# A gated DeltaNet kernel on one core: an urgency for each stage of a unit, norm weights spread by TensorE, and the first and last state products left out

## The chip, the cores and the metric

The kernel runs on one core of a Trainium2 chip. The metric is the device time of one execution in microseconds (us), as the median of three runs. The kernel before takes 1268.69 us (1267.94 to 1268.84).

## The reference, cut to what matters

A model dimension of 1024, 2048 tokens, one layer of a gated DeltaNet with 8 heads of 128, and a final RMSNorm. Everything is float32. The parts that the change touches are the first norm and the chunked recurrence:

```python
h = x + gated_deltanet_mixer(rms_norm(x, a_norm_w), ...)   # then rms_norm(h, final_norm_w)

proj = h @ w_in                                   # q, k, v, z, and two gates per head
qkv  = silu(causal_depthwise_conv(qkv, conv_w))   # 4 taps
...
def step(state, xs):                              # one chunk of one head
    u_c, w_c, qd_c, kend_c, attn_c, gend_c = xs
    v_new = u_c - w_c @ state
    o_c = qd_c @ state + attn_c @ v_new
    state = state * gend_c[..., None, None] + jnp.swapaxes(kend_c, -1, -2) @ v_new
    return state, o_c

s0 = jnp.zeros((b_, h_, dk, dv), jnp.float32)
_, o = lax.scan(step, s0, (u, w, q_decayed, k_to_end, attn_intra, g_end))
y = rms_norm(o, o_norm_w) * silu(z)               # then y @ w_out
```

The state starts at zero, and the state after the last chunk is not an output. (The kernel uses chunks of 128 tokens.)

## The kernel before, in words

The work is cut into 16 units: 2 halves of the sequence (1024 tokens each) times 8 heads. A unit has these stages, each a function of its own. `project` (line 649) multiplies the normalised tokens by the head's slice of the weights, for k, q, v and z (KI, QI, VI, ZI), in two blocks of 512 tokens each. Tokens and weights are each split into a rounded part and its remainder (xh and xl, hi and lo), so a block of one kind is 24 matmuls of 512 columns. `conv_block` (622) does the convolution and SiLU. `decay` (664) makes the decay matrices, `k_side` (678) what depends on k and q alone, `invert` (723) the triangular inverse V, mostly as a long chain of small VectorE steps followed by four rounds of small matmuls, `v_side` (778) turns v, and `recur` (789) runs the 8 chunks of the recurrence one after the other, each reading the state S that the chunk before it left.

Ahead of unit 0 and again ahead of unit 8, `phase0` (512) loads and normalises the half's eight tiles of 128 tokens (`norm_tile`, 481), transposes them on TensorE and splits them; `gates` (543) follows. In `norm_tile` an even tile is scaled by one VectorE instruction (scale and norm weight at once), an odd one by ScalarE (scale) and then GpSimd (norm weight). After unit 15, `out_tile` (863) multiplies by the output weights; its first tiles are woven into the last units.

None of this is issued as it is written. Every call goes into a `Plan` (line 20), which records the operation with its dependencies and with `nc.prio`, the number set last before the call. `Plan.schedule` (193) then runs a list scheduler over the recorded operations with a cost table of its own: whenever an engine is free by its reckoning, it takes the ready operation with the lowest number (ties go to the one recorded first), unless a buffer is missing or the operation is more than `AHEAD` = 2.0 behind the most urgent one that is left. What comes out is one fixed order for each engine, and the engines keep to it. So `nc.prio` does not say when something runs. It only sets the order in each engine's queue, and a wrong reckoning shows as a wait of an engine for the head of its queue.

Before, the numbers are the unit's own number u for nearly everything of unit u, and u - 0.5 for `invert` and for the second half's norm and gates (lines 915 to 937):

```python
nc.prio = float(u)
...
nc.prio = u - 0.5
invert(un)
nc.prio = float(u)
project(un, ((VI, 0), ...))
v_side(un)
```

`recur(prev)` of unit u - 1 is recorded in round u with number u. Every instruction is emitted by line 354, so the profile's rows are told apart by their tiles: `xh,rnd` and `xl,rnd` are projections (rnd holds weights), `ident,big` transposes of the normalised tokens, `S`, `rho` and `n` belong to the recurrence (S is the state, `n` and `rho` are a chunk's intermediate results), `T` and `V` to the inverse, `half` is any tile of 512 columns, `bank` any PSUM bank. A float32 matmul stands in the trace as two instructions, one for each pass; a projection (float32r) as one.

## Time and profile before

| what | before |
|---|---|
| median of three runs | 1268.69 us |
| the profiled execution, its own time | 1271.77 us |
| its span, first to last instruction | 1270.0 us |
| TensorE (PE) busy | 1242.9 us |
| VectorE (DVE) busy | 954.2 us |
| ScalarE (ACT) busy | 615.5 us |
| GpSimd (POOL) busy | 173.0 us |
| mean granted TensorE clock | 0.988 |

The profiled execution's span is 1.3 us above the median of the runs. Busy time of PE includes the time in which one matmul drains while the next one already runs, so a stretch with 100% may still hold short waits. The granted clock has two levels, 1.00 (2.4 GHz) and 0.50 (1.2 GHz); a value in between is a mean over a stretch.

### The profile page before, as it was taken

The numbers are of one execution on the slowest core, as the hardware profiler recorded it, in microseconds if no ns is written. First come the engines' busy times: TensorE is split into PE (matmuls) and PEld (weight loads), VectorE is DVE, ScalarE is ACT, GpSimd is POOL, SyncE is SP. The second block draws the span as 40 slices with busy tenths as digits, with TensorE's granted clock in tenths as the row PEclk, the third lists the DMA queues.
The fourth block names the chain that finished last, engine by engine and source line by source line (L and its number), as shares of the span: only waits on it lengthen the run. The fifth ranks groups of instructions, "written<-read, shape, count | busy, mean of one in ns | idle before, by whom it ended". The sixth has DMA issues, their size and how long they took to land.

```text
span 1270.0 us, 21157 instructions
## 1 busy us (share of the span) xinstructions
PE 1242.9 (98%) x8093; PEld 1039.9 (82%) x8093; DVE 954.2 (75%) x2229; ACT 615.5 (48%) x1301; POOL 173.0 (14%) x277
## 2 busy tenths in 40 slices
PE   6999999999999999989999999999999999999997
PEld 5788788888888888878888888888888888888886
DVE  5678867887877869776787878787878698965653
ACT  6664364545455445556554545454545455232221
POOL 5211011101112102130110202020202010100000
PEclk9999899999999999989999999999999999999999
DMA  7130313122242131313302222222223316255721
GB/s 223 34 114 24 107 43 104 51 80 83 63 112 77 49 93 48 121 42 102 113 3 77 61 78 61 78 62 78 61 77 111 110 60 211 96 201 190 277 100 67
DMA packets 127623, 118.80 MB, mean 94 GB/s; under 512 B 24001, under 2 KB 106530, under 8 KB 127522
## 3 DMA queue, kind: packets, MB, share of 16 engines
q1 hardware_dynamic: 127522, 117.45, 30.3%
q8 instruction: 63, 1.03, 0.3%
q14 instruction: 38, 0.31, 0.1%
HBM read 98.36 MB, written 19.07 MB: 92 GB/s over the span
## 4 chain that ended last, share of the span: by engine, by line
PE 96%; DVE 2%; ACT 1%; DMA 0%; issue 0%; POOL 0%; SPq 0%; POOLq 0%; DVEq 0%; ACTq 0%
PE bank L354 96%; DVE half L354 1%; DMA big<-in_a_norm_w_dram 0%; DVE big L354 0%; ACT xh L354 0%; DVE xl L354 0%; ACT half L354 0%; POOL big L354 0%; DVE X L354 0%; ACT rnd L354 0%; DVE rnd L354 0%; ACT big L354 0%; SPq L354 0%; ACT n L354 0%; DVE sumo L354 0%
## 5 line engine op out<-in xcount | busy, mean ns | idle before, releaser
L354 PE MATMUL bank<-xh,rnd 128*128 128x512 f32 (+1 forms) x2624 | 884.1, 405 | 2.8 <-ACT rnd L354 1.7
L354 PEld LDWEIGHTS bank<-xh,rnd 128*128 128x128 f32 x2624 | 485.0, 190 | 91.5 <-ACT rnd L354 1.9
L354 PE MATMUL bank<-xl,rnd 128*128 128x512 f32 (+1 forms) x1328 | 535.0, 403 | 0.8 <-DVE xl L354 0.8
L354 PEld LDWEIGHTS bank<-xl,rnd 128*128 128x128 f32 x1328 | 253.4, 191 | 44.9 <-DVE xl L354 1.5
L354 DVE SCALAR_TENSOR_TENSOR half<-raw,vcol,half 128x512 f32<-128x512 f32 x288 | 211.8, 746 | 39.2 <-ACT half L354 37.0
L354 ACT ACTIVATE half<-half 128x512 f32<-128x512 f32 x128 | 81.6, 638 | 99.8 <-DVE half L354 98.2
L354 ACT CAST rnd<-big 128x1024 fp32r<-128x1024 f32 x80 | 83.8, 1050 | 76.3 <-PE bank L354 64.2
L354 ACT COPY raw<-bank 128x512 f32<-128x512 f32 x96 | 56.5, 588 | 118.9 <-PE bank L354 118.2
L354 ACT ACTIVATE n<-bank,nb 128x128 f32<-128x128 f32 x128 | 46.9, 366 | 131.2 <-PE bank L354 131.0
L354 DVE TENSOR_TENSOR rnd<-big,rnd 128x1024 fp32r<-128x1024 f32 x80 | 97.7, 1221 | 17.0 <-ACT rnd L354 14.2
L354 DVE TENSOR_TENSOR half<-X,big 128x6 f32<-128x6 f32 (+15 forms) x256 | 94.2, 368 | 4.4
L354 DVE TENSOR_REDUCE X<-half 128x2 f32<-128x6 f32 (+15 forms) x256 | 91.9, 359 | 3.7
L354 DVE SCALAR_TENSOR_TENSOR S<-S,dend,bank 128x128 f32<-128x128 f32 x128 | 44.1, 344 | 61.1 <-PE bank L354 60.2
L354 POOL COPY halo<-raw 128x3 f32<-128x3 f32 x72 | 21.5, 299 | 478.8 <-ACT raw L354 478.8
L354 ACT ACTIVATE half<-big 128x512 bf16<-128x512 f32 (+1 forms) x48 | 37.0, 772 | 81.5 <-issue 38.5
L354 ACT ACTIVATE half<-raw,vcol 128x512 f32<-128x512 f32 x96 | 69.6, 725 | 6.2 <-DVE vcol L354 1.5
L354 DVE SCALAR_TENSOR_TENSOR rho<-bank,eg,half 128x128 f32<-128x128 f32 x128 | 44.2, 345 | 25.6 <-PE bank L354 25.0
L354 PEld LDWEIGHTS bank<-rho,V 128*128 128x128 f32 x256 | 47.8, 191 | 11.9 <-ACT V L354 0.8
L354 PEld LDWEIGHTS bank<-n,half 128*128 128x128 f32 x256 | 47.5, 190 | 11.4 <-ACT n L354 1.4
L354 PEld LDWEIGHTS bank<-S,half 128*128 128x128 f32 x256 | 47.2, 191 | 11.2 <-DVE S L354 1.7
L354 POOL TENSOR_TENSOR sk<-ssk,phalf 128x4 f32<-128x4 f32 x32 | 39.5, 1233 | 123.2 <-DVE ssk L354 123.2
L354 ACT ACT_TABLE_LOAD x42 | 53.9, 1283 | 1.5 <-PEq L968 0.7
(114 smaller groups left out, 1583.2 us busy)
## 6 DMA issues: line engine op xcount, KB each, us to landing
big<-in_a_w_in_dram SPq DMA_DIRECT2D x64, 512.0 KB, 4.5
big<-in_x_dram SPq DMA_DIRECT2D x32, 512.0 KB, 4.1
big<-gd SPq DMA_DIRECT2D x16, 512.0 KB, 6.3
half<-gd SPq DMA_DIRECT2D x32, 256.0 KB, 4.3
big<-d SPq DMA_DIRECT2D x16, 512.0 KB, 5.4
yd<-half SPq DMA_DIRECT2D x32, 256.0 KB, 2.3
big<-yd SPq DMA_DIRECT2D x16, 512.0 KB
big<-rd SPq DMA_DIRECT2D x16, 512.0 KB, 4.5
```

The lines of the kernel that those rows point to most:

```text
L354: ins = getattr(getattr(self.tc.nc, op[6]), op[7])(*args, **kwargs)
```

## The change

There are three edits. First, each stage gets a number of its own relative to u, from a table `AT`; the projections of z are recorded separately from those of v, with u - 0.58, and weight loads get another -0.14. In the last unit of a half the gates get u - 0.31 in place of u - 0.5. Second, `a_norm_w` is no longer loaded into all 128 partitions by a DMA that reads the row 128 times. One row is loaded into partition 0, two matmuls with a row of ones spread it over the partitions, and two VectorE copies bring it back from PSUM. This holds for the first half; the second half's norm loads the weights as before. With it go smaller edits to the start: the first eight tiles are all scaled by VectorE, the very first in two halves. Third, the chunk that starts from the zero state (chunk 0 of units 0 to 7) issues no k S, no S qe, and copies instead of updating S, and the states are no longer cleared; the last chunk of units 8 to 15 doesn't update S at all.

```diff
+AT = dict(kq0=-0.25, kq1=-0.09, decay=0.0, k0=0.0, k1=-0.07, inv=-0.36, v=0.0, z=-0.58, vside=-0.67, phase=-0.5,
+          gates=-0.31, w=-0.14)
...
-    nws = [weights_row(a_norm_w)]
+    nc.prio = -1.1
+    ones = cp.tile([P, P], F32, name="ones")
+    nc.vector.memset(ones, 1.0)
+    nws = [st([P, D], F32, "nw")]
+    nc.sync.dma_start(nws[0][0:1], a_norm_w)
+    for c0 in range(0, D, TB):
+        pw = ps("nt")
+        nc.tensor.matmul(pw, lhsT=ones[0:1], rhs=nws[0][0:1, c0:c0 + TB], start=True, stop=True)
+        nc.vector.tensor_copy(nws[0][:, c0:c0 + TB], pw)
...
-    for h in range(H):
-        nc.gpsimd.memset(state[h], 0.0)
...
-        if t % 2:
+        if t % 2 and i >= len(x_first):
             nc.scalar.mul(xt, xt, rs)
             nc.gpsimd.tensor_tensor(out=xt, in0=xt, in1=nw, op=ALU.mult)
         else:
-            nc.vector.scalar_tensor_tensor(out=xt, in0=xt, scalar=rs, in1=nw, op0=ALU.mult, op1=ALU.mult)
+            for c0 in range(0, D, TB if i == 0 else D):
+                cols = slice(c0, c0 + (TB if i == 0 else D))
+                nc.vector.scalar_tensor_tensor(out=xt[:, cols], in0=xt[:, cols], scalar=rs, in1=nw[:, cols],
+                                               op0=ALU.mult, op1=ALU.mult)
...
+        at = nc.prio
+        if at >= 1:
+            nc.prio = at + AT["w"]
         nc.sync.dma_start(raw, w_in[:, c0:c0 + P].rearrange("(k p) c -> p k c", p=P))
         split_w(raw, hi, lo)
+        nc.prio = at
...
+            begin, end = un["sb"] == 0 and cc == 0, un["sb"] == NSB - 1 and cc == C - 1
             pch = ps("ch", (P, 3, P))
-            nc.tensor.matmul(pch[:, 0, :], lhsT=k[:, cs], rhs=S, start=True, stop=True)
             rho = st([P, P], F32, "rho")
-            nc.vector.scalar_tensor_tensor(out=rho, in0=pch[:, 0, :], scalar=gt["eg"][:, h, cc:cc + 1], in1=vp[:, cs],
-                                           op0=ALU.mult, op1=ALU.subtract)
+            if begin:
+                nc.vector.tensor_scalar_mul(rho, vp[:, cs], -1.0)
+            else:
+                nc.tensor.matmul(pch[:, 0, :], lhsT=k[:, cs], rhs=S, start=True, stop=True)
+                nc.vector.scalar_tensor_tensor(out=rho, in0=pch[:, 0, :], scalar=gt["eg"][:, h, cc:cc + 1],
+                                               in1=vp[:, cs], op0=ALU.mult, op1=ALU.subtract)
             nc.tensor.matmul(pch[:, 1, :], lhsT=V[:, cc, :], rhs=rho, start=True, stop=True)
             n = st([P, P], F32, "n")
             nc.scalar.mul(n, pch[:, 1, :], un["nb"][:, cc:cc + 1])
-            nc.tensor.matmul(po[:, c * P:(c + 1) * P], lhsT=S, rhs=qe[:, cs], start=True, stop=False)
-            nc.tensor.matmul(pch[:, 2, :], lhsT=kend[:, cs], rhs=n, start=True, stop=True)
-            nc.vector.scalar_tensor_tensor(out=S, in0=S, scalar=gt["dend"][:, h, cc:cc + 1], in1=pch[:, 2, :],
-                                           op0=ALU.mult, op1=ALU.add)
-            nc.tensor.matmul(po[:, c * P:(c + 1) * P], lhsT=n, rhs=att[:, cs], start=False, stop=True)
+            if not begin:
+                nc.tensor.matmul(po[:, c * P:(c + 1) * P], lhsT=S, rhs=qe[:, cs], start=True, stop=False)
+            if not end:
+                nc.tensor.matmul(pch[:, 2, :], lhsT=kend[:, cs], rhs=n, start=True, stop=True)
+            if begin:
+                nc.vector.tensor_copy(S, pch[:, 2, :])
+            elif not end:
+                nc.vector.scalar_tensor_tensor(out=S, in0=S, scalar=gt["dend"][:, h, cc:cc + 1], in1=pch[:, 2, :],
+                                               op0=ALU.mult, op1=ALU.add)
+            nc.tensor.matmul(po[:, c * P:(c + 1) * P], lhsT=n, rhs=att[:, cs], start=begin, stop=True)
...
-        nc.prio = float(u)
+        nc.prio = u + AT["decay"]
         decay(un)
+        nc.prio = u + AT["k0"]
         k_side(un, 0)
...
-        nc.prio = u - 0.5
+        nc.prio = u + AT["inv"]
         invert(un)
...
```

What the numbers do is seen in the order of TensorE's queue. The first place is its very beginning; `ident,big` are the transposes of the first two token tiles. Before:

```order
L980 UNCONDITIONAL_BRANCH
L354 MATMUL bank_165<-ident,big_101 128x128 x4
L354 MATMUL bank_170<-ident,big_101 128x128 x4
L354 MATMUL bank_184<-ident,big_106 128x128 x4
L354 MATMUL bank_189<-ident,big_106 128x128 x4
L354 MATMUL bank_199<-xh_173,rnd_182 128x256
```

And now:

```order
L1015 UNCONDITIONAL_BRANCH
L357 MATMUL bank_122<-big_101,ones 128x512
L357 MATMUL bank_129<-big_101,ones 128x512
L357 MATMUL bank_159<-ident,big_106 128x128 x4
L357 MATMUL bank_167<-ident,big_106 128x128 x4
L357 MATMUL bank_181<-ident,big_110 128x128 x4
L357 MATMUL bank_189<-ident,big_110 128x128 x4
L357 MATMUL bank_203<-xh_169,rnd_177 128x256
L357 MATMUL bank_203<-xl_179,rnd_177 128x256
```

The two matmuls that spread the norm weights stand ahead of the transposes; nothing else moved here.

The second place is the end of unit 0's inverse (`T` or `V` with 64x64) and its first chunks (`V` with rho, n, S). Before:

```order
L354 MATMUL bank_165<-V_85,half_705 64x64 x8
L354 MATMUL bank_189<-rho_835,V_85 128x128
L354 MATMUL bank_189<-n_1300,half_631 128x128
L354 MATMUL bank_199<-half_758,n_1300 128x128
L354 MATMUL bank_184<-S_76,half_439 128x128
L354 MATMUL bank_199<-half_680,S_76 128x128
L354 MATMUL bank_184<-rho_1312,V_85 128x128
L354 MATMUL bank_184<-n_1317,half_631 128x128
L354 MATMUL bank_199<-half_758,n_1317 128x128
L354 MATMUL bank_242<-S_76,half_439 128x128
L354 MATMUL bank_199<-half_680,S_76 128x128
L354 MATMUL bank_236<-xh_173,rnd_258 128x512
```

And now:

```order
L357 MATMUL bank_129<-rho_859,V_85 128x128
L357 MATMUL bank_181<-xl_361,rnd_177 128x512
L357 MATMUL bank_122<-ident,half_431 128x128 x4
L357 MATMUL bank_181<-xh_352,rnd_193 128x512
L357 MATMUL bank_181<-xh_352,rnd_177 128x512
L357 MATMUL bank_129<-n_1254,half_680 128x128
L357 MATMUL bank_203<-half_774,n_1254 128x128
L357 MATMUL bank_181<-xl_361,rnd_177 128x512
L357 MATMUL bank_181<-xh_352,rnd_193 128x512
L357 MATMUL bank_181<-xh_352,rnd_177 128x512
L357 MATMUL bank_167<-S_76,half_446 128x128
L357 MATMUL bank_203<-half_641,S_76 128x128
```

Before, ten products of the recurrence stood one behind the other, without a projection between them, most of them waiting for the result of an earlier one by way of another engine; now three projections of unit 1 stand between one step and the next, once with four transposes among them. Counted in the whole order, 13 projection matmuls stood between the end of unit 0's inverse and the start of unit 1's; now 119 do.

The third place is the end of the second half's norm, just ahead of unit 7's inverse (`T` with 32x32; `ident,big` are the norm's transposes). Before:

```order
L354 MATMUL bank_165<-xh_173,rnd_489 128x512
L354 MATMUL bank_189<-ident,big_131 128x128 x4
L354 MATMUL bank_170<-ident,big_131 128x128 x4
L354 MATMUL bank_165<-xl_179,rnd_489 128x512
L354 MATMUL bank_184<-T_84,big_106 32x32 x16
```

And now:

```order
L357 MATMUL bank_181<-xh_352,rnd_99 128x512
L357 MATMUL bank_203<-xh_169,rnd_247 128x512
L357 MATMUL bank_203<-xl_179,rnd_247 128x512
L357 MATMUL bank_203<-xh_169,rnd_177 128x512
L357 MATMUL bank_167<-T_84,big_113 32x32 x16
L357 MATMUL bank_203<-xh_169,rnd_247 128x512
L357 MATMUL bank_203<-xl_179,rnd_247 128x512
```

Before, 26 projection matmuls of unit 8 stood ahead of unit 7's inverse, the last two between the transposes of the norm; now 75 do, z among them. The transposes of the norm's last tile, which stood inside the inverse, have moved ahead of it with the others.

## Rows read from the trace of the kernel before

**Rows 1.** Page, parts 1 and 4: busy time by engine; the chain that ended last.

```profile
PE 1242.9 (98%) x8093; PEld 1039.9 (82%) x8093; DVE 954.2 (75%) x2229; ACT 615.5 (48%) x1301; POOL 173.0 (14%) x277
...
PE 96%; DVE 2%; ACT 1%; DMA 0%; issue 0%; POOL 0%; SPq 0%; POOLq 0%; DVEq 0%; ACTq 0%
```

**Rows 2.** Windows by stage: start:end, length, busy us by engine, PEclk, DMA.

```profile
0.00:20.00 20.00, 9.56 (x48) 8.32 (x48) 8.12 (x19) 12.33 (x19) 11.28 (x28) 1.00 0.93 284
20.00:40.00 20.00, 17.66 (x133) 16.31 (x133) 11.96 (x23) 14.05 (x25) 9.46 (x10) 1.00 0.38 108
40.00:60.00 20.00, 19.76 (x91) 16.08 (x92) 15.43 (x39) 12.59 (x25) 3.03 (x4) 0.91 0.05 16
160.00:240.00 80.00, 80.00 (x501) 68.31 (x502) 62.70 (x148) 41.46 (x94) 12.87 (x22) 1.00 0.27 78
1250.00:1270.00 20.00, 12.67 (x56) 10.13 (x54) 6.13 (x13) 2.17 (x6) 1.10 (x2) 0.92 0.13 52
```

**Rows 3.** Windows, the last stage, projections of the output alone.

```profile
1210.00:1220.00 10.00, 10.00 (x45) 8.12 (x44) 4.98 (x10) 2.32 (x5) 1.40 (x1) 1.00 0.30 107
```

**Rows 4.** Timeline of PE: start us, busy us, operation.

```profile
528.08 0.38 PE L354 MATMUL bank<-rho,V 128*128 128x128 f32 x2
528.22 0.48 PE L354 MATMUL bank<-xl,rnd 128*128 128x512 f32 x1
528.54 0.63 PE L354 MATMUL bank<-xh,rnd 128*128 128x512 f32 x2
529.00 0.40 PE L354 MATMUL bank<-xl,rnd 128*128 128x512 f32 x1
```

**Rows 5.** Page, part 5: groups of instructions, busy us and mean ns.

```profile
L354 PE MATMUL bank<-xh,rnd 128*128 128x512 f32 (+1 forms) x2624 | 884.1, 405 | 2.8 <-ACT rnd L354 1.7
...
L354 DVE TENSOR_REDUCE X<-half 128x2 f32<-128x6 f32 (+15 forms) x256 | 91.9, 359 | 3.7
```

**Rows 6.** Timeline of the start, all engines.

```profile
1.65 0.42 SPq L354 DMA_DIRECT2D big<-in_a_norm_w_dram  x1
...
4.18 1.06 ACT L354 ACTIVATE half<-big 128x1024 bf16<-128x1024 f32 x1 [2.17 <-DMA big<-in_x_dram]
...
6.19 1.20 POOL L354 TENSOR_TENSOR rs<-ss,nhalf 128x1 f32<-128x1 f32 x2
...
7.70 1.28 DVE L354 SCALAR_TENSOR_TENSOR big<-big,rs,big 128x1024 f32<-128x1024 f32 x1 [0.94 <-DMA big<-in_a_norm_w_dram]
8.65 2.54 POOL L354 TENSOR_TENSOR big<-big,big 128x1024 f32<-128x1024 f32 x1 [1.26 <-ACT big L354]
...
9.04 1.97 PE L354 MATMUL bank<-ident,big 128*128 128x128 f32 x8 [9.04 <-DVE big L354]
```

**Rows 7.** Windows around the first unit's recurrence, as in rows 2.

```profile
136.00:140.00 4.00, 3.10 (x36) 2.41 (x35) 3.62 (x12) 1.16 (x2) 0.00 (x0) 1.00 0.03 6
140.00:144.00 4.00, 2.42 (x10) 1.93 (x9) 3.70 (x8) 0.37 (x1) 0.00 (x0) 0.53 0.00 0
144.00:148.00 4.00, 3.35 (x13) 2.47 (x13) 3.75 (x8) 2.25 (x3) 0.00 (x0) 0.50 0.30 86
148.00:152.00 4.00, 4.00 (x15) 3.25 (x15) 3.83 (x10) 0.66 (x2) 0.00 (x0) 0.69 0.37 110
```

**Rows 8.** Windows around the second half's norm.

```profile
544.00:552.00 8.00, 7.11 (x40) 5.63 (x39) 7.50 (x15) 6.08 (x12) 2.17 (x2) 1.00 0.57 166
552.00:560.00 8.00, 5.29 (x101) 4.14 (x100) 7.80 (x18) 5.06 (x10) 3.22 (x4) 1.00 0.00 0
560.00:568.00 8.00, 8.00 (x44) 5.84 (x43) 4.85 (x8) 1.75 (x3) 2.08 (x1) 0.51 0.01 2
568.00:576.00 8.00, 8.00 (x39) 6.33 (x38) 1.74 (x3) 3.44 (x5) 0.00 (x0) 0.64 0.00 1
```

**Rows 9.** Windows at the end of the first norm.

```profile
36.00:40.00 4.00, 2.96 (x22) 2.28 (x20) 2.47 (x6) 1.59 (x3) 1.38 (x1) 1.00 0.72 190
40.00:46.00 6.00, 5.76 (x17) 4.36 (x18) 5.10 (x8) 4.04 (x7) 1.25 (x2) 0.72 0.17 50
```

More of the change, by code (lines that the diff above doesn't have):

```diff
@@ L396, in tile_gated_deltanet @@
     for t, tag in enumerate(("E", "U", "A", "xin", "xin", "E", "U", "A")):
-        nc.prio = (-1.0, -0.99, -0.96, -0.95, -0.8, -0.79, -0.78, -0.77)[t]
+        nc.prio = (-1.0, -0.975, -0.96, -0.95, -0.8, -0.79, -0.78, -0.77)[t]
         xt = st([P, D], F32, tag)
@@ L422, in tile_gated_deltanet @@
     nc.vector.tensor_scalar_mul(nexpA, nexpA, -1.0)
-    ones = cp.tile([P, P], F32, name="ones")
-    nc.vector.memset(ones, 1.0)
     phalf = cp.tile([P, C], F32, name="phalf")
@@ L917, in tile_gated_deltanet @@
             recur(prev)
-        if u == 0:
-            nc.prio = -0.72
+        nc.prio = u + AT["kq0"] if u else -0.72
         project(un, ((KI, 0), (QI, 0)), 2 if u == 0 else 1)
-        nc.prio = float(u)
+        nc.prio = u + AT["decay"]
         decay(un)
+        nc.prio = u + AT["k0"]
         k_side(un, 0)
+        nc.prio = u + AT["kq1"]
         project(un, ((KI, 1), (QI, 1)))
+        nc.prio = u + AT["k1"]
         k_side(un, 1)
-        nc.prio = u - 0.5
+        nc.prio = u + AT["inv"]
         invert(un)
-        nc.prio = float(u)
-        project(un, ((VI, 0), (ZI, 0), (VI, 1), (ZI, 1)) if last else ((VI, 0), (VI, 1), (ZI, 0), (ZI, 1)))
+        if last:
+            nc.prio = u + AT["v"]
+            project(un, ((VI, 0), (ZI, 0), (VI, 1), (ZI, 1)))
+        else:
+            nc.prio = u + AT["v"]
+            project(un, ((VI, 0), (VI, 1)))
+            nc.prio = u + AT["z"]
+            project(un, ((ZI, 0), (ZI, 1)))
+        nc.prio = u + AT["vside"]
         v_side(un)
         if last and u < NU - 1:
-            nc.prio = u - 0.5
+            nc.prio = u + AT["phase"]
             xhs, xls, pba = phase0(u // H + 1)
+            nc.prio = u + AT["gates"]
             gt = gates(pba)
```

## The prediction, made before the changed kernel was run

> **What bounds the kernel now.** I read the page first, then the busy times by stage, then the three places where TensorE (PE) is not full, and last the start.
>
> The page shows PE busy for 1242.9 of 1270.0 us and on 96% of the chain that ended last [rows 1]. In a stage in the middle of the kernel, from 160 to 240 us, PE is busy for 80.00 of 80 us at clock 1.00, VectorE (DVE) for 62.70 [rows 2]. So whatever is taken from PE there comes off the time, and nothing taken from another engine does. The reader is to see in the rows by stage that the 27.1 us without PE work lie in few places: 9.0 us before its first transposes [rows 6], 2.7 us more up to 36 us (what is left of the 10.44 and 2.34 us in the first two stages after 9.04 and the 1.04 us counted next) [rows 2, 6, 9], 1.3 us from 36 to 46 us [rows 9], 3.1 us from 136 to 152 us [rows 7], 3.6 us from 544 to 560 us [rows 8], and 7.3 us at the end [rows 2], after the last matmul.
>
> The last three inner places cost more than their idle time, because the granted clock is at its lower level, 0.50, behind each. PE had waited again and again in the stretch before. A clock of 0.53 over 4 us means 3.8 us at that level; in this way rows 7 hold 3.8 + 4.0 + 2.5 = 10.2 us of it. PE was busy for about 8 of them at half the rate, which loses 4.0 us; with the 3.1 us idle this place, call it A, loses 7.1 us. Rows 8 hold 7.8 + 5.8 = 13.6 us at the lower level, all of it busy: 6.8 us lost, and with 3.6 us idle place B loses 10.4 us. Rows 9 hold 0.28 x 2 x 6 = 3.4 us: 1.7 us lost, 1.3 us idle; with the 2.7 us before it, place C loses 5.7 us.
>
> At A, PE has little else in its queue than the chunk chain of unit 0, and unit 1's inverse follows after 13 projection matmuls (3 us). DVE is busy for 3.62 to 3.83 of each 4 us [rows 7]. The reductions of all 16 inverses take 91.9 us [rows 5], 5.7 us for one, and each has a multiplication beside it: what PE gets as cover between the two inverses is far shorter than what DVE needs for the second. At B, DVE is busy for 7.50 and 7.80 of 8 us [rows 8], with unit 7's inverse, the norm's tiles and the gates all due at once.
>
> The Trainium skill ("Perfetto Trace Analysis", section "Identifying the Most-Contended Engine") says that matmul busy time is a bad measure of how full TensorE is, and that the busy share of weight loads is a better one. By that rule the 82% on the page would leave 18% free, the 5.5 us of the first step below could be hidden, and the sum would be 17.4 us. The trace answers it: in a stretch of bare projections without one wait the share is 8.12 of 10 us [rows 3], so 82% is what a full queue shows in this kernel, and I keep the 5.5 us.
>
> **The products left out.** Eight units issue two products less and eight issue one less: 24. What one costs is seen where it stands between projections: rho times V and the projection behind it take 0.46 us from start to start (528.08 to 528.54), and two projections also take 0.46 us (528.54 to 529.00), so a projection takes 0.23 us and a product 0.23 us [rows 4]. 24 x 0.23 = 5.5 us, all on PE. Nothing hides them, since only the four of units 0 and 7 lie in places (A and B) where PE is not full. On DVE the eight updates become copies and the eight combinations become scalings of the same size: nothing. The eight cleared states leave GpSimd's (POOL's) queue, ahead of its first power (below).
>
> **The start.** The weights' load into all partitions was issued at 1.65 us and ended the wait of the first scaling, at 7.70 us, after 0.94 us of idle time; the transposes began at 9.04 us [rows 6]. In the new kernel that scaling waits for its own chain. The row's load is first in SP's queue, ahead of the two token tiles, so x comes one issue (0.42 us) later: the square that began at 4.18 us begins at 4.6 us. It takes 1.06 us. Its read-out, a DVE step and POOL's power took 1.5 us more (5.24 to 6.79 us; POOL's two powers stand as 1.20 us from 6.19 us [rows 6]), which would put the scaling at 7.2 us. But POOL, whose clears stood ahead of the power, has eight less of them; I take 6.8 us. Half a scaling is about 0.6 us, and transposes begin near 7.4 us: 1.6 us earlier. Two things come on top. The second tile goes from ScalarE and POOL (2.54 us for POOL's part [rows 6]) to one DVE scaling of 1.28 us, and the loads that share the DMA engines (busy share 0.93 in this stage [rows 2]) have 0.5 MB less beside them. I take 1.8 us, with ends at 0 (if another load sets the first projection) and 4 us.
>
> The spreading itself does not stand in the trace of before. Lower end: nothing, as it lies beside x's load and square. Upper end: two float32 matmuls of 512 columns are four instructions, 4 x 0.41 us by the nearest row [rows 5] = 1.6 us, and half a DVE scaling for each copy, 2 x 0.7 us, one behind the other: 3.0 us. If the row lands as late as x did, 3.4 us after its issue, the weights are ready at 4.2 + 3.0 = 7.2 us, 0.4 us after the scaling could begin. I take nothing, as a row of 4 KB has less to move than the tile; without that cover it is 0.4 us. On PE the two matmuls stand ahead of the transposes, which have nothing to do until 6.8 us anyway. What is queued behind their copies on DVE is the first tile's own step.
>
> **The urgencies.** At A the order now puts 119 projection matmuls (27 us) between the two inverses in place of 13, and three between the chunk steps where there were none. DVE needs two times 5.7 us and its share of convolutions in that time, which fits. I count all of A's 7.1 us; ends 0 and 7.1.
>
> At B 75 projection matmuls of unit 8 stand ahead of unit 7's inverse in place of 26: 49 x 0.23 = 11.3 us more for DVE to get through the norm and the inverse. The idle time was 3.6 us, so the time is there if it falls at the right moment. But DVE is nearly full over the whole stretch, its work there is the same, and PE's order has several transposes of the norm that wait for DVE one by one. I take 7 of 10.4 us, with ends 0 and 10.4.
>
> At C the order of the last tiles, the transposed convolution weights and the gate columns is much as it was; what shortens is the path of the odd tiles, and DVE carries four scalings of 1.28 us more in exchange. I take 1.5 of 5.7 us, with ends -2 (DVE was busy for 5.10 of 6 us [rows 9]) and 5.7.
>
> In the stretches where PE is full, a new order of the same work can't save anything, and costs whatever new waits it makes. The nearest rows say none (80.00 of 80), and that order was made by the same planner with the same costs, so I take 0. Weight loads come 0.14 earlier in urgency; SP's queue has room for them (POOL and SP are nowhere on the chain [rows 1]).
>
> **The sum.** 5.5 + 1.8 + 7.1 + 7 + 1.5 = 22.9 us. Against the profiled span of 1270.0 us that is 1247.1 us; the median of the runs lies 1.3 us under that span, which gives 1245.8 us, so 1246 us. All places at their better ends give 5.5 + 4 + 7.1 + 10.4 + 5.7 = 32.7 us less, 1236 us.
>
> **The rivals.**
>
> The stalls stay (1261 us): DVE, not the order, sets A and B, the new order waits at another row for the same result, and only the products and the start are gained: 1268.7 - 7.3 = 1261.4 us. For it: DVE is over 90% busy in both places. Against it: at A the cover between the two inverses grows ninefold, and over whole stages DVE has a fifth of its time free (62.70 of 80 us [rows 2]).
>
> Nothing comes of it (1268 us): the gains of products and start are eaten by one new stall. A stall of 3 us with the clock's fall behind it cost 7.1 us at A, so one of that kind is enough if A and B also stay. Against it: two things must happen together.
>
> Slower (1278 us or more): a wait in every unit. The z projections, which were the filler at the end of a unit, now run before the unit's own k and q; `k_side`, and with it the inverse, come later against the recurrence that needs it. If PE then waits at the first round of each inverse, that is one wait in each of some 13 units that have none now. It decides from 22.9 / 13 = 1.8 us for each; at 2.5 us, 1246 + 32 = 1278 us, and with the clock falling behind each wait, as at A, three units already cancel the gain. For it: the inverse is a long chain of small DVE steps, and tiles for z are held longer. Against it: counted in the order, 119 to 216 projections stood between one inverse and the next from unit 2 to unit 7 before, without a wait in the stage from 160 to 240 us [rows 2], and 136 to 188 stand there now. The Trainium skill ("Perfetto Trace Analysis", section "Identifying Performance Opportunities", under its optimization strategy) reads the same gap again and again on the engine that should be full as a sign that buffers have run out; z held longer would do that here. The trace of before has no such gap in that stage, and no trace yet shows the longer hold.
>
> **How the numbers follow.** The forecast, with A gone and B at least half gone: 0.66, with its own range from 1238 to 1254 us. Stalls stay, or one of them and a new small one: 0.20, 1254 to 1265 us. Nothing: 0.07. Slower: 0.07. Two in ten may be left out, so the range reaches from 1238 to 1261 us. About 0.2% (2.5 us) is what can be told from no change: faster 0.88, same 0.05, slower 0.07.
>
> **What the new profile would show.** Right: PE's first transposes near 7.4 us; 48 PE instructions fewer for the products and 4 more for the spreading; no stretch at the lower clock level behind the first recurrence, and a shorter one or none where the second half's norm ends; 80 of 80 us in the middle. Wrong: PE waiting for DVE in every unit ahead of the 32x32 matmuls of the inverse; or A's place quiet and the same idle time at another one; or the first transposes still near 9 us, behind the copies of the spread weights.

## The result, and the profile after

The changed kernel takes 1240.9 us (median of four runs, 1240.69 to 1241.15), the kernel before 1268.62 us in the same comparison: a ratio of 0.978 with an interval from 0.9765 to 0.9794, 27.7 us less. The forecast was 1246 us, from 1238 to 1261. So the sign, the range and the likeliest case hold, and the gain is 4.8 us larger than the sum.

The page of the changed kernel, parts 1 and 4, answers to [rows 1]:

```profile
PE 1225.3 (99%) x8049; PEld 1024.5 (83%) x8049; DVE 962.2 (78%) x2228; ACT 607.5 (49%) x1297; POOL 170.5 (14%) x265
...
PE 98%; ACT 1%; DVE 1%; issue 0%; DMA 0%; POOLq 0%; POOL 0%; DVEq 0%; ACTq 0%
```

PE has 44 instructions less: 48 for the products, and 4 for the spreading on top. Its idle time fell from 27.1 to 13.9 us (1239.2 - 1225.3). All of PE's waits of the changed kernel, by what they waited for (us in total, times, longest):

```profile
PE bank L357 <- DVE big L357: 3.0, 2, 2.3
PE bank L357 <- DMA big<-in_a_norm_w_dram: 2.3, 1, 2.3
PE bank L357 <- ACT xh L357: 0.7, 2, 0.5
PE bank L357 <- ACT half L357: 0.4, 1, 0.4
```

All but 0.7 us of these waits lies in the first 14 us. The windows of the places A, B and C, the same stretches as in [rows 7], [rows 8] and [rows 9] (start:end, length, busy us of PE, PEld, DVE, ACT, POOL, then PEclk and DMA):

```profile
136.00:140.00 4.00, 4.00 (x23) 3.44 (x22) 3.69 (x6) 1.71 (x4) 0.43 (x1) 1.00 0.88 288
140.00:144.00 4.00, 4.00 (x26) 3.53 (x25) 3.26 (x13) 2.94 (x4) 0.00 (x0) 1.00 0.02 8
144.00:148.00 4.00, 4.00 (x23) 3.40 (x22) 3.66 (x14) 1.56 (x4) 0.00 (x0) 1.00 0.00 0
```
```profile
544.00:552.00 8.00, 8.00 (x39) 6.22 (x38) 7.88 (x16) 3.62 (x5) 0.69 (x3) 1.00 0.17 43
552.00:560.00 8.00, 8.00 (x119) 6.07 (x118) 7.21 (x22) 5.08 (x9) 0.00 (x0) 1.00 0.34 90
560.00:568.00 8.00, 8.00 (x53) 6.40 (x51) 4.59 (x15) 6.75 (x11) 0.56 (x3) 1.00 0.01 2
```
```profile
36.00:40.00 4.00, 3.76 (x19) 2.76 (x18) 3.15 (x7) 2.59 (x5) 0.00 (x0) 1.00 0.01 2
40.00:46.00 6.00, 6.00 (x29) 4.64 (x28) 5.96 (x10) 5.28 (x7) 1.13 (x2) 1.00 0.01 3
```

PE is full at each but for 0.24 us at C, at clock 1.00, while DVE is about as busy as before (7.88 and 7.21 of 8 us at B, 7.50 and 7.80 before). The start answers to [rows 6]:

```profile
0.74 0.34 SPq L357 DMA_DIRECT2D big<-in_a_norm_w_dram  x1
...
2.27 3.75 PE L357 MATMUL bank<-big,ones 1*128 1x512 f32 x4 [2.27 <-DMA big<-in_a_norm_w_dram]
...
4.55 1.06 ACT L357 ACTIVATE half<-big 128x1024 bf16<-128x1024 f32 x1 [2.53 <-DMA big<-in_x_dram]
...
6.05 0.69 DVE L357 COPY big<-bank 128x512 f32<-128x512 f32 x1 [0.72 <-PE bank L357]
6.66 0.14 DVE L357 TENSOR_SCALAR ss<-ss 128x1 f32<-128x1 f32 x1
...
8.28 1.97 PE L357 MATMUL bank<-ident,big 128*128 128x128 f32 x8 [2.27 <-DVE big L357]
...
13.39 0.58 PE L357 MATMUL bank<-xh,rnd 128*128 128x256 f32 x1 [0.47 <-ACT xh L357]
```

The four spreading instructions take 3.75 us, the second copy comes at 6.05 us, and the first tile's ss, which is ready when its square is read out (5.70 us), stands behind it. The transposes begin at 8.28 us, 0.8 us earlier than before. The first projection doesn't gain by it: it begins at 13.39 us, against 13.11 us before, and the second at 14.12 against 14.48 us. What the start gains beyond that comes later, at the rounded weights (see C below).

### The profile page after: what moved, and what is told of

It reads as the page before. It is cut to its first block, busy times and chain, and to the rows that moved or that the text cites. A ratio compares the mean times of both kernels' runs of the same rounds, so it can differ in the third digit from the quotient of the medians.

```text
span 1239.2 us, 21069 instructions
## 1 busy us (share of the span) xinstructions
PE 1225.3 (99%) x8049; PEld 1024.5 (83%) x8049; DVE 962.2 (78%) x2228; ACT 607.5 (49%) x1297; POOL 170.5 (14%) x265
## 4 chain that ended last, share of the span: by engine, by line
PE 98%; ACT 1%; DVE 1%; issue 0%; DMA 0%; POOLq 0%; POOL 0%; DVEq 0%; ACTq 0%
PE bank L357 98%; ACT half L357 0%; DVE big L357 0%; ACT rnd L357 0%; DVE half L357 0%; DMA big<-in_a_norm_w_dram 0%; ACT L357 0%; DVE rnd L357 0%; ACT xh L357 0%; ACT big L357 0%; DVE xl L357 0%; POOLq L1015 0%; POOL rs L357 0%; ACT raw L357 0%; DVEq L1015 0%
## 5 line engine op out<-in xcount | busy, mean ns | idle before, releaser
L357 PE MATMUL bank<-xh,rnd 128*128 128x512 f32 (+1 forms) x2624 | 871.8, 402 | 0.7 <-ACT xh L357 0.7
L357 DVE SCALAR_TENSOR_TENSOR rho<-bank,eg,half 128x128 f32<-128x128 f32 x120 | 41.6, 347 | 27.3 <-PE bank L357 26.9
L357 DVE SCALAR_TENSOR_TENSOR S<-S,dend,bank 128x128 f32<-128x128 f32 x112 | 38.6, 345 | 26.0 <-PE bank L357 25.0
L357 POOL TENSOR_TENSOR rs<-ss,nhalf 128x1 f32<-128x1 f32 x32 | 23.6, 737 | 252.3 <-DVE ss L357 245.0
L357 DVE TENSOR_TENSOR big<-bank,big 128x512 f32<-128x512 f32 x32 | 22.1, 691 | 45.2 <-PE bank L357 45.2
```

Of the source, the lines that this page charges most:

```text
L357: ins = getattr(getattr(self.tc.nc, op[6]), op[7])(*args, **kwargs)
```

## The experiments

Two theories. **Cover:** what decides is how many projection matmuls the order puts between one inverse and the next, and ahead of unit 7's inverse; the three parts of the change then add up. **Lottery:** the places with waits are a property of each whole order; every edit gives another order, which has stalls of its own, and the changed kernel's order is one that has almost none. Each experiment was timed beside the kernel before, whose median was 1268.3 to 1269.5 us there; its single executions spread from 1265.9 to 1272.5 us, those of the changed kernel only from 1240.69 to 1241.15. Differences under some 2 us between two experiments rest on their traces. Counts of projections between the first two inverses run from here on from the first round of one inverse to the first round of the next: 28 before and 134 in the changed kernel, 15 more than the 13 and 119 counted from the end of unit 0's inverse.

**The urgencies alone.**

```diff
 kernel before
+AT = dict(kq0=-0.25, ..., w=-0.14), and its uses in load_w and in the loop over the units
```

> The kernel before with the new urgencies alone: old start, all products. Theory (cover): 140 projection matmuls stand between the first two inverses in place of 28, and 71 of unit 8 ahead of unit 7's inverse in place of 26, so places A and B fill and the clock stays at 1.00 from 60 us on: 7.1 + 10.4 us, and about 3 us of short waits beside them that count as busy in the trace, so 1268.6 - 20 = 1248 us (1246 to 1252). Rival (A and B went because the chain of unit 0 and the row of DVE work got shorter with the products and the start): A or B still shows the lower clock level, and the time is 1256 us or more.

Measured: 1259.15 us, ratio 0.9916 (0.9899 to 0.9934), 9.8 us less. By the number, and by a rest of the lower clock at A, this is the rival's result, but not for the rival's reason: with all products and the old start A shrank to waits of 1.6 and 0.2 us with 3.4 us at the lower clock behind them, and B's long stretch at the lower level is gone. What is left of the time lies in new waits, among them 1.4 us at 525 us and 1.6 us at 542 us, and in the waits up to 46 us, which are no shorter than they were. PE's waits from 60 us on:

```profile
PE bank L357 <- DVE S L357: 1.8, 2, 1.6
PE bank L357 <- DVE rho L357: 1.6, 1, 1.6
PE bank L357 <- DVE big L357: 1.4, 1, 1.4
```

**The products alone, in the old order.**

```diff
 kernel before, its order unchanged
-matmul(pch[:, 0, :], k, S); matmul(po, S, qe)      # at the first chunk
-matmul(pch[:, 2, :], kend, n)                      # at the last chunk
+rho = -vp;  S = pch[:, 2, :];  matmul(po, n, att, start=True)   # at the first chunk
```

> The kernel before in its own order, instruction for instruction, with the 24 products on the zero state and for the final state left out, the eight first combinations as scalings and the eight first updates as copies. Theory (PE is full): 24 x 0.23 = 5.5 us less, perhaps up to 0.9 us less of that where the four products of units 0 and 7 lie in places with waits: 1263 us (1262.5 to 1264.5). Rival (a full PE has room at 82% of weight loads): 0 to 2 us less, 1267 to 1268.6 us. Places A and B keep their lower clock in both.

Measured: 1263.88 us, 0.9958 (0.9943 to 0.9973), 5.1 us less (3.4 to 7.2 by the interval). A full PE pays for the products: compared projection by projection with the trace of before, from 600 to 1190 us, this run gains eight times 0.22 to 0.25 us, one step for each product that is left out there.

The trace also shows that this order doesn't cost the same in every execution. B's stretch at the lower clock is 3.4 us here, where it was 13.6 us in [rows 8], and B costs 5.8 us in place of 10.4. And the start is 3.2 us later: the norm weights landed 1 us later and released the first tile's scaling on DVE together with GpSimd's multiplication of the second tile, and the scaling took 3.44 us in place of the 1.28 us in [rows 6]:

```profile
8.73 3.44 DVE L361 SCALAR_TENSOR_TENSOR big<-big,rs,big 128x1024 f32<-128x1024 f32 x1 [2.11 <-DMA big<-in_a_norm_w_dram]
8.75 2.34 POOL L361 TENSOR_TENSOR big<-big,big 128x1024 f32<-128x1024 f32 x1 [1.48 <-DMA big<-in_a_norm_w_dram]
```

The first transposes began at 12.22 us, against 9.04. In the changed kernel the first tiles are not multiplied on GpSimd, so this can't happen at its start.

**The start alone.**

```diff
 kernel before
+row of a_norm_w, two matmuls with ones, two copies; first eight tiles scaled on DVE
-load of a_norm_w into all partitions; odd first tiles on ScalarE and GpSimd
```

> The kernel before with the edits of the start alone (weights spread by TensorE, the first eight tiles scaled on DVE, the clears of the states kept): old urgencies, all products. Theory (cover): the start gains under 1 us, since the two matmuls take 3.75 us and the second copy stands ahead of the first tile's step; place C gains 3 to 5 us; the planner now puts 72 projection matmuls between the first two inverses (28 before), 16.6 us for twice 5.7 us of reductions and as much again in multiplications, so A shrinks in part; B has 26 matmuls of unit 8 as before and stays. 1268.6 - 0.5 - 4 - 3.5 = 1260.5 us (1257 to 1265). Rival (A and C went by the urgencies): only the start's 0 to 2 us, 1267 to 1268.6 us.

Measured: 1269.7 us, 0.9997 (0.9986 to 1.0007). I missed by 9 us. C and A did what the cover theory said: C is full (3.76 of 4 and 6.00 of 6 us busy), A has no lower clock left, with 72 projections where there were 28. B stays as expected, in another form: waits of 1.5 us (534 us) and 6.1 us with 6.8 us at the lower clock, some 11 us in all for 10.4. But the new order brings a stall that the old one did not have, 2.4 us at 494 us with 10.2 us at the lower clock behind it, some 7.5 us. PE's waits from 485 to 575 us, and the longest of them in PE's timeline:

```profile
PE bank L354 <- DVE T L354: 8.6, 3, 6.1
PE bank L354 <- DVE big L354: 1.5, 1, 1.5
```
```profile
553.53 0.39 PE L354 MATMUL bank<-half,S 128*128 128x128 f32 x2
560.00 0.31 PE L354 MATMUL bank<-T,big 32*32 32x32 f32 x2 [6.08 <-DVE T L354]
```

`T` is the tile that the first round of the inverse (32x32) and its third (64x64) read: PE stands 6.08 us at the first round of unit 7's inverse, and the 2.4 us at 494 us are at the third round of unit 6's.

**The z urgencies alone.**

```diff
 the kernel with the new urgencies alone
-AT = dict(kq0=-0.25, kq1=-0.09, ..., inv=-0.36, v=0.0, z=-0.58, vside=-0.67, ...)
+AT = dict(kq0=0.0, kq1=0.0, ..., inv=-0.5, v=0.0, z=-0.58, vside=-0.67, ...)
```

> The kernel before with only the urgency of a unit's z projections and of its v side moved (-0.58 and -0.67; weight loads, inverse, norm and the rest as before). Theory (cover): 126 projection matmuls stand between the first two inverses in place of 28, so A goes (7.1 us and about 1 us of short waits beside it); ahead of unit 7's inverse stand 26 matmuls of unit 8 as before, so B stays with its lower clock: 1268.6 - 8 = 1260.5 us (1258 to 1263). Rivals: z early cures both places, 1250 us; or it moves the stalls and the time stays at 1268 us.

Measured: 1282.44 us, 1.0097 (1.0079 to 1.0116), 13.5 us slower. A is full, as forecast (4.00 of 4 us in each window from 136 to 152 us). But from 60 us on PE waits seven times for `T`, a tile of an inverse:

```profile
PE bank L357 <- DVE T L357: 11.8, 7, 5.2
PE bank L357 <- ACT half L357: 3.4, 3, 1.9
```

The long ones are 4.5 and 5.2 us at the first rounds of units 6 and 7 and 1.3 us at the third of unit 14. The lower clock lies at all three places, for 10.2, 6.8 and 13.7 us. This is the mechanism of the prediction's slower rival, though at three units and not in every one: with z early alone an inverse comes late against PE. With the whole table (the urgencies alone, above) PE has no wait for `T`.

**The changed kernel without the start's edits.**

```diff
 kernel after
-the start's edits (row, matmuls, copies, first eight tiles on DVE)
+load of a_norm_w into all partitions; odd first tiles on ScalarE and GpSimd
```

> The changed kernel with the edits of the start undone (weights loaded into all partitions by the DMA, odd first tiles on ScalarE and GpSimd, eight clears of the states are still left out); the planner then gives another order up to unit 8 and the same counts of projections between inverses from there on (142 between the first two, 75 of unit 8 ahead of unit 7's inverse). Theory 1 (cover by these counts): no stretch at the lower clock after 60 us; the start and place C cost again what the urgencies' own run had more there, 1.1 + 2.6 + 1.2 = 4.9 us and 1 us of clock: 1241 + 6 = 1247 us (1245 to 1249). Theory 2 (every order of the planner brings stalls of its own, and that of the changed kernel is one that has none): besides the 6 us one to three stalls between 60 and 600 us, 1250 to 1260 us.

Measured: 1253.16 us, 0.9873 (0.9858 to 0.9888), the second theory's number. Urgencies and products together give 16.3 us less, close to 9.8 + 5.1; the start, which alone gave nothing, is worth 12.3 us here. About half of the loss, some 6.5 us by the projections at 90 us, is at the start and at C, where it was counted; the other half is not. PE waited 1.37 us at 522 us and 1.62 us at 540 us, as in the first run, and DVE's timeline shows why; below it GpSimd's in the same stretches:

```profile
520.17 3.41 DVE L357 SCALAR_TENSOR_TENSOR big<-big,rs,big 128x1024 f32<-128x1024 f32 x1 [0.67 <-POOL rs L357]
...
538.53 2.42 DVE L357 TENSOR_TENSOR half<-X,big 128x104 f32<-128x104 f32 x1
```
```profile
520.10 2.40 POOL L357 TENSOR_TENSOR big<-big,big 128x1024 f32<-128x1024 f32 x1
...
537.40 3.43 POOL L357 TENSOR_TENSOR big<-big,big 128x1024 f32<-128x1024 f32 x1 [1.65 <-ACT big L357]
```

A scaling that takes 1.28 us elsewhere takes 3.41 us here, and a multiplication of 104 elements 2.42 us in place of 0.26: the first ends 1.1 us, about its own duration, behind GpSimd's multiplication of an odd tile by the norm weights (522.50 us), the second 0.1 us behind the next (540.83 us).

**The same, with GpSimd's part moved to DVE.**

```diff
 after_old_start, its order unchanged
-nc.gpsimd.tensor_tensor(out=xt, in0=xt, in1=nw, op=ALU.mult)   # second half's odd tiles
+nc.vector.tensor_tensor(out=xt, in0=xt, in1=nw, op=ALU.mult)   # at the same place
```

> The run after_old_start in its own order, with the multiplications of the second half's odd norm tiles by the weights issued on DVE at the places in the program order where GpSimd had them. In after_old_start a scaling on DVE took 3.41 us in place of 1.28 beside such a multiplication (POOL busy from 520.10 us) and a 104-element multiplication 2.42 us in place of 0.26 beside another (from 537.40 us), and PE waited 1.37 and 1.62 us right behind. Theory (POOL's long multiplication holds DVE's operations of two SBUF inputs): both waits go, 1253.2 - 3.0 = 1250 us (1249.3 to 1251.3). Rival (DVE is simply full there): the four multiplications cost DVE 4 x 1.2 us more and the waits stay or grow, 1253 us or more.

Measured: 1251.02 us, 0.986 (0.9843 to 0.9877). The first theory's number. The span of the profiled execution fell from 1252.0 to 1249.2 us although DVE has four multiplications more. Of these 2.8 us, 0.9 are there by 90 us, ahead of the edit, where PE waited 2.55 us for the rounded weights in after_old_start and 1.67 us here, in the same order; 1.9 us come between 520 and 561 us. Each run has four executions, and their times overlap (1248.88 to 1253.04 us against 1251.13 to 1254.28), so the evidence is in the rows. The same operations on DVE:

```profile
519.25 1.28 DVE L358 SCALAR_TENSOR_TENSOR big<-big,rs,big 128x1024 f32<-128x1024 f32 x1 [0.67 <-POOL rs L358]
520.50 1.19 DVE L358 TENSOR_TENSOR big<-big,big 128x1024 f32<-128x1024 f32 x1
...
536.52 0.26 DVE L358 TENSOR_TENSOR half<-X,big 128x104 f32<-128x104 f32 x1
```

1.28 in place of 3.41 us, and 0.26 in place of 2.42; PE's two waits are 0.22 and 0.34 us. So GpSimd's multiplication of two SBUF tiles and DVE's operations with two SBUF inputs hold each other off. The Trainium skill ("SBUF — State Buffer", section "Who interferes with whom") states that a DVE instruction with two SBUF inputs contends with a GpSimd instruction that reads SBUF, and calls this contention an exclusive lock; the two pairs of rows agree.

**z late, and the inverse early, in the changed kernel.**

```diff
 kernel after
-z=-0.58, vside=-0.67          |    -inv=-0.36
+z=0.0, vside=0.0              |    +inv=-0.5
```

> The changed kernel with the urgencies of a unit's z projections and v side put back to 0. Between the first two inverses stand 108 projection matmuls (134 in the changed kernel, 28 before), ahead of unit 7's inverse 57 of unit 8 (75, 26). Theory 1 (cover by these counts): A is free of waits, B costs at most a third of its 10.4 us: 1241 to 1245 us. Theory 2 (an order is a lottery of stalls): 1248 to 1262 us, with waits of PE for the first round of an inverse at other units. Theory 3 (z early is what keeps PE fed behind each recurrence): waits in most units and 1260 us or more.

Measured: 1245.23 us, 0.9814 (0.9801 to 0.9828), 0.2 us over the first theory's range. Most of the gain stays, so z's early urgency is not what removes A and B. It has waits of about 1 us at 541, 544 and 1070 us that the changed kernel has not; the one at 541 us is again behind a DVE operation stretched beside GpSimd's multiplication (2.36 us in place of 0.18).

> The changed kernel with the urgency of the inverse at -0.5 as before in place of -0.36, the same as that of the second half's norm. 154 projections between the first two inverses, 48 of unit 8 ahead of unit 7's inverse, but none between the norm's last transposes and that inverse (31 in the changed kernel). Theory 1 (cover): A free, B waits at the norm or at the inverse with the lower clock behind it, about half of 10.4 us: 1246 us (1243 to 1250), and no other waits. Theory 2 (a lottery of stalls): waits at other units too, 1250 to 1262 us.

Measured: 1255.59 us, 0.9898 (0.9884 to 0.9912). 14.7 us of the gain are gone with one number. B is back, and longer than in [rows 8]:

```profile
544.00:552.00 8.00, 4.27 (x22) 3.08 (x20) 7.93 (x14) 3.20 (x5) 3.77 (x4) 0.94 0.00 0
552.00:560.00 8.00, 5.22 (x89) 4.05 (x89) 6.79 (x15) 4.05 (x9) 0.00 (x0) 0.50 0.30 78
560.00:568.00 8.00, 8.00 (x30) 5.64 (x29) 0.42 (x1) 1.62 (x2) 0.00 (x0) 0.50 0.08 23
```

The time is the second theory's, but most of the loss is at B, where the first put it. 48 projections of unit 8 stand ahead of unit 7's inverse, almost twice the 26 of before, and it did not help: none stands between the norm's last transposes and the inverse, so norm, inverse and gates still fall due together. With 31 (the changed kernel), 34 (the neighbour, below) or 9 (z late) there, the lower clock does not appear. So at B the inverse's place behind the norm seems to count for more than the number that I counted. The runs don't separate the two fully, since every order with such a gap also has 56 projections of unit 8 or more ahead.

Nor do they separate the place from the clash with GpSimd, which stands in this order too, right in the inverse's chain on DVE (`X`), the last of its multiplications among them:

```profile
548.71 2.57 DVE L357 TENSOR_TENSOR half<-X,big 128x256 f32<-128x256 f32 x1
```
```profile
548.62 2.38 POOL L357 TENSOR_TENSOR big<-big,big 128x1024 f32<-128x1024 f32 x1 [0.90 <-ACT big L357]
```

This multiplication takes 0.42 us elsewhere. It takes 2.15 us longer here, and PE's wait for the first round of this inverse is 2.6 us. The same order without GpSimd's part was not run.

**The changed kernel with 24 products put back, in its own order.**

```diff
 kernel after, its order unchanged
+matmul(pch[:, 0, :], k, vp); matmul(po, vp, qe)    # at the first chunk
+matmul(pch[:, 2, :], kend, n)                      # at the last chunk, read by nothing
```

> The changed kernel in its own order, instruction for instruction, with a product of the same size issued at each of the 24 places where the change left one out (k with vp, vp with qe, kend with n; their results are overwritten or not read). If a full PE pays for every product, 5.5 us more than the changed kernel: 1246.4 us (1245.5 to 1247), with no stretch at the lower clock after 20 us. If the order alone made the difference and PE has room, 1241 to 1242.5 us. If the change's freedom from stalls rests on the shorter chains, stalls come back at A or B and it is over 1250 us.

Measured: 1246.18 us, 0.9821 (0.9808 to 0.9835), 5.3 us more than the changed kernel, and no wait from 60 to 1200 us. So the products are worth 5.1 and 5.3 us in the two orders, the second with little spread (1245.76 to 1247.1 us), and the changed kernel's freedom from stalls belongs to its order, not to the shorter chains.

**The weights by one DMA, in the changed kernel's order.**

```diff
 kernel after, its order unchanged
-dma_start(nws[0][0:1], a_norm_w); two matmuls; two copies
+dma_start(nws[0], a_norm_w.broadcast_to([P, D]))
```

> The changed kernel in its own order, with the norm weights loaded into all 128 partitions by one DMA at the place of the row's, first in SP's queue, and the two spreading matmuls and their copies left out. Theory 1 (only the moment of the weights counts): the load of 0.5 MB stands ahead of x's tiles and puts them off by less than a microsecond, and DVE's first step no longer stands behind the second copy (0.6 us): 1240.5 to 1241.8 us, no difference that can be told. Theory 2 (the spreading by TensorE is what the start gains by): first transposes at 9 us or later in place of 8.28, and 1242 us or more.

Measured: 1242.76 us, 0.9796 (0.9782 to 0.981); span 1241.0 us against 1239.2. The start of it:

```profile
6.53 1.06 ACT L360 ACTIVATE half<-big 128x1024 bf16<-128x1024 f32 x1 [4.52 <-DMA big<-in_x_dram]
...
7.71 0.15 DVE L360 TENSOR_SCALAR ss<-ss 128x1 f32<-128x1 f32 x1 [2.38 <-ACT half L360]
...
9.35 1.97 PE L360 MATMUL bank<-ident,big 128*128 128x128 f32 x8 [9.35 <-DVE big L360]
```

The second theory. The first tile's square, which waits for x alone, begins at 6.53 us in place of 4.55: with 0.5 MB ahead of it x is usable 2.0 us later than with a row of 4 KB ahead of it, where the first theory had less than 1 us. Only 1.05 us of this shows at ss (7.71 for 6.66 us), as ss stands behind the second copy in the changed kernel. Against this variant the spreading is worth 1.1 us at the first transposes and 1.8 us of span, in a fixed order. In the kernel before, x stood ahead of the weights and its square began at 4.18 us; so against that kernel x doesn't come earlier.

**A neighbour: one urgency moved by 0.02.**

```diff
 kernel after
-decay=0.0
+decay=-0.02
```

> The changed kernel with one urgency moved by 0.02: the decay of a unit stands at -0.02 in place of 0.0, ahead of its k side and v projections where it was level with them. The order is the same up to unit 2; 134 projections between the first two inverses as in the changed kernel, 56 of unit 8 ahead of unit 7's inverse (75), 34 between the norm's last transposes and that inverse (31). Theory 1 (cover by counts): 1241 to 1243 us. Theory 2 (an order is a lottery of stalls): at least one wait of over 1 us between 300 and 600 us and 1244 to 1256 us.

Measured: 1247.49 us, 0.9838 (0.9822 to 0.9854), 6.6 us over the changed kernel; the second theory. PE's waits from 60 us on:

```profile
PE bank L357 <- DVE S L357: 1.1, 1, 1.1
PE bank L357 <- DVE rho L357: 1.1, 1, 1.1
PE bank L357 <- DVE xl L357: 0.4, 2, 0.2
```

At 529 us four of DVE's subtractions for the norm (xl, 0.69 us each) stand ahead of a chunk's update and the next chunk's rho. By the count of projections done it is 4.6 us behind at 548 us, 1.2 at 640 and 6.0 at 1190 us; as the orders differ, such a count is rough. From 560 us on no wait of the trace names the loss. It stays open.

**A quicker start.**

```diff
 kernel after, its order unchanged but for the first 14 us
+second copy behind ss (missed, see below); second tile scaled in two halves;
+third tile's square behind the high part of the second tile's first half
```

> The changed kernel in its own order but for the first 14 us: the second copy of the spread weights goes behind the first tile's ss on DVE, the first tile's second half behind the second tile's ss, the second tile is scaled in two halves, and on ScalarE the third tile's square goes behind the high part of the second tile's first half. By its rows ss is ready near 5.7 us and stood until 6.66 us, so the first scaling comes 0.7 us earlier, the second tile's transposes 1 to 2 us earlier, and the first projection at 12.3 us in place of 13.39. If nothing but this chain sets the start: 1 us less than the changed kernel, 1239.9 us (1239.4 to 1240.5). If the low part of the first weights (ready at 13.24 us) or the tiles 3 and 4 set it, no gain: 1240.9 us.

Measured: 1240.68 us (1240.35 to 1240.91), 0.9779 (0.9765 to 0.9792); not to be told from the changed kernel. The first of its moves named a wrong instruction: in the trace the second copy still stands at 6.07 us and ss at 6.68 us. The others worked, and met the low part of the first weights, as the second expectation said:

```profile
12.38 0.58 PE L372 MATMUL bank<-xh,rnd 128*128 128x256 f32 x1 [0.19 <-ACT xh L372]
...
13.81 0.58 PE L372 MATMUL bank<-xl,rnd 128*128 128x256 f32 x1 [0.86 <-DVE ss L372]
```

The first projection came 1.0 us earlier, the second 0.3 us (14.12 us in the changed kernel), because DVE makes the weights' low part ahead of the tile's. What the missed move is worth was not tried.

## Why the prediction was right, and where it was not

Point by point, PE's idle time and half of what it was busy at the lower clock, before and after, from the two profiled executions:

| term | forecast | found | shown by |
|---|---|---|---|
| 24 products | 5.5 | 5.1 to 5.3 | two runs in fixed orders |
| start, to the first transposes | 1.8 | 0.8 | 9.04 to 8.28 us |
| C, with the 2.7 us before it | 1.5 | 4.1 | 5.7 to 1.6 us |
| A | 7.1 | 7.1 | 3.1 idle and 4.0 of clock, to nothing |
| B | 7 | 10.0 | 10.4 to 0.43 us |

With 5.5 for the products that is 27.5 us of the 30.8 us by which the two profiled spans differ; the other 3.3 us are not found. That the sum comes out near the 27.7 us between the medians is chance: the profiled execution of before was 3.1 us above its median, and A, B and the start are not the same in every execution of it (B cost 10.4 us here and 5.8 us in the run with the products left out).

**The products** were sized rightly. The rule that I weighed against them, by which the 18% without a weight load are room, falls: two different orders paid the full price.

**The start** was mis-sized in the step on the spreading. Its upper bound, 4 x 0.41 + 2 x 0.7 = 3.0 us, was no bound: the four instructions took 3.75 us, 0.94 each, where I took a projection's 0.41 us for a float32 instruction of as many columns in a stretch in which PE had done nothing before. The second copy then stood in front of the first tile's ss, where I had "the first tile's own step" queued behind the copies and cost it at nothing: ss was ready to run at 5.70 us and ran at 6.66, which is most of the 0.9 us by which the transposes missed the forecast 7.4 us. Not in the sum at all is that the old start can come out 3.2 us later (12.22 us for 9.04, in the run with the products left out), which the new one can't.

**C** failed in the sizing. I wrote "what shortens is the path of the odd tiles, and DVE carries four scalings of 1.28 us more in exchange", and took 1.5. The largest part that rows name is on ScalarE: with the old start PE waits 1.7 us (kernel before) to 2.6 us (urgencies alone, and urgencies with products) for `rnd`, the rounded weights on ScalarE, and has no such wait in the changed kernel. Before, this cast stands behind an odd tile's scaling, which itself waits for GpSimd's rs:

```profile
17.83 1.15 ACT L354 ACTIVATE big<-big,rs 128x1024 f32<-128x1024 f32 x1 [1.91 <-POOL rs L354]
...
20.19 1.06 ACT L354 CAST rnd<-big 128x1024 fp32r<-128x1024 f32 x1
...
21.30 0.39 PE L354 MATMUL bank<-xh,rnd 128*128 128x256 f32 x1 [1.67 <-ACT rnd L354]
```

In the changed kernel ScalarE has lost the odd tiles' scaling and makes this cast at 14.76 us. Runs show that C belongs to the start: it is full with the start's edits alone, not with the urgencies alone. It is also full with the weights by one DMA, so it belongs to the tiles' move to DVE or to the order that comes with it, not to the spreading. Which step held C itself, from 36 to 46 us, no run shows.

**A** went by the cover, as argued: 72, 126 or 140 projections between the first two inverses, by three different edits, left at most 1.8 us of waits around it, and the 10 us at the lower clock of [rows 7] shrank to nothing, or to 3.4 us with the urgencies alone.

**B** came out larger than 7 us, and the 49 more projections are not the whole reason. One number decides it in this kernel: the inverse's -0.36 behind the norm's -0.5. Put back to -0.5 it costs 14.7 us, with 22 more projections ahead than before. Whether the gap behind the norm does it by itself, or by keeping the inverse's steps on DVE out of GpSimd's multiplications, stays open.

**New waits: 0** was right for the changed kernel and wrong as reasoning, so here the forecast was lucky. I argued that the same planner with the same costs makes no new waits where PE was full. Start alone, z alone, the neighbour and the inverse alone each show that it does: from 2.6 us of waits after 60 us (the neighbour) to 17.4 us (z alone, 11.8 + 3.4 + 1.1 + 0.9 + 0.2), where the kernel before has 6.6 us and the changed one 0.4. In five of the seven other orders (urgencies alone, start alone, without the start's edits, z late, inverse early) PE waits 1.1 to 1.6 us behind a DVE operation that took 2.4 to 3.4 us beside GpSimd's multiplication; in the changed kernel the largest such excess is 0.65 us (at 515.8 us), and no wait stands behind it. The planner's costs hold nothing for the clock that falls behind many of the waits. It does keep such operations of GpSimd and DVE apart, but only in its own reckoning of time. So the parts do not add: 9.8 + 5.1 - 0.7 = 14.2 us apart, 27.7 us together. Of the 12.3 us that the start brings on top of the others, some 6.5 us are there by the projections at 90 us (1.8 of them from the spreading, by the run with one DMA), and some 5 us come between the projections at 476 and 548 us, where GpSimd and DVE hold each other off in the one order and hardly in the other; 1.9 us of these are shown to be theirs, by the run with GpSimd's part on DVE. These two figures compare counts of projections in two orders and are rough. A chance of 0.07 for "slower" looks too low for a change of this kind: of the seven other orders of the planner that were run, one was 13.5 us slower than before, one the same and five faster by 10 to 24 us, none as fast as the changed kernel.

## What to carry to other kernels

Where a planner sets the order, size an edit twice: in a frozen order, which gives its own price, and through the planner, which gives the price and the stalls of a new order; only the first can be put down to the edit itself. Behind a wait on TensorE look at the two engines that feed it, first for a step that takes longer than its like (3.41 us for 1.28), then for what stands ahead in that queue. Stages that are due together want an order among themselves and not only cover: at B, twice the cover without the order gained nothing.

## What the runs showed of the hardware

- A float32 matmul of one row by 512 columns in a stretch where PE had been idle took 1.88 us (3.75 us for two, four instructions), against 0.23 us for a float32r projection of 128 rows and as many columns later. The granted clock reads 1.00 at both places, though the same eight transposes took 1.97 us at 9.04 us and 1.04 us at 18.6 us in the kernel before.
- DVE's and GpSimd's instructions with two SBUF inputs stretch each other: 1.28 to 3.41 us and 0.26 to 2.42 us on DVE, and 2.40 to 3.43 us on GpSimd, beside a DVE operation of 1.22 us.
- A load of 0.5 MB to all partitions ahead of a tile of the same size delayed the step that needs the tile by 2.0 us (4.55 to 6.53 us), against a row of 4 KB ahead of it.
- In one and the same order at the start, weights that landed 1 us later brought a DVE and a GpSimd operation together and moved TensorE's first transposes from 9.04 to 12.22 us.
